# Seven block products in place of eight for half of the channel mixer's second product

## The chip, the cores and the metric

The kernel runs on one NeuronCore of a Trainium2 chip. The metric is the device time of one execution in microseconds (us), lower is better; the median of three runs stands for it.

## The reference

The reference is a trunk of two layers over 256 tokens of 2048 channels. What the change touches is the channel mixer that ends each token mixer:

```python
for i in range(DEPTH):                # DEPTH = 2, D_FF = 8192
    ...
    h = rms_norm(x, mlp_norm[i])
    x = x + jnp.square(jax.nn.relu(h @ mlp_w1[i])) @ mlp_w2[i]
    g = jax.nn.sigmoid(rms_norm(x, ple_norm[i]) @ ple_w_gate[i])
    x = x + g * (p[i] @ ple_w_proj[i])
return rms_norm(x, final_norm)
```

`mlp_w1` is 2048x8192 and `mlp_w2` 8192x2048 in each layer; tokens and weights are float32.

## The kernel before, in words

**Divided operands.** TensorE gets every float32 operand as a high part and a low part (type float32r), and each product is three passes: high by high, high by low, low by high (`PASSES_W_MOVES`). The class `Weights` streams the weights: a tile of 128x2048 float32 (1 MB: 512 rows by 512 columns of the matrix) is loaded by SyncE's DMA queue into a `raw` buffer (`load`, L61; three buffers), ScalarE copies it to the high half of an `hl` buffer (`divide`, L75; four buffers), and VectorE subtracts that from the raw tile to make the low half (L76). This pair is called a split below. `next` hands out the tiles in order and keeps three of them split ahead of the one in use. The order of TensorE's and SyncE's instructions is the order in which the code issues them; ScalarE's and VectorE's is set by the tile framework's scheduler when the program is built. Each engine runs its queue strictly in that order, and semaphores hold an instruction until its inputs are ready and its output buffer is free.

**The channel mixer.** The 8192 hidden channels are 16 chunks q of 512, taken in pairs f = 0 to 7. `w1` (L523, L528) makes a chunk in two PSUM tiles with the weights standing and the tokens moving; ScalarE and VectorE bring it out (L538 to L543): low columns added, relu, square, divided into a high and a low part `h`. `w2` multiplies a pair of chunks by the columns of `mlp_w2`, four column groups n of 512 channels, two weight tiles and 48 matmuls of 128x512 for each (`rows_product`, L297), and VectorE adds the PSUM result, scaled by the squared inverse norm, to the residual `x` (`add_to_x`, L320). The loop runs w1(f), then w2(f-1), so that TensorE always has a product whose inputs are old. After the last pair, `after.chunk(n)` squares the finished column group of x and, some matmuls later, transposes it on TensorE (L275) for the gate product of `embed` that comes next.

A **round** below is what TensorE does for one pair: two chunks of w1 (8 tiles) and the four column groups of w2 (8 tiles). There are 8 rounds in a layer and 16 in all.

## Time and profile before

| what | value |
|---|---|
| median of 3 runs (lowest, highest) | 1995.26 us (1995.0, 1995.62) |
| the profiled execution's own time | 1994.55 us |
| its span, first to last instruction | 1992.8 us |
| TensorE matmuls busy | 1972.8 us, 99% of the span, 9918 matmuls |
| VectorE busy | 1166.5 us, 59% |
| ScalarE busy | 932.2 us, 47% |
| weights read | 373.75 MB, 189 GB/s over the span |
| granted TensorE clock, mean | 0.998 of full speed |

The profile is of one execution. Busy time of an engine is the time in which an instruction of it runs; since matmuls are pipelined, a busy TensorE is not one at its peak. The view by lines groups equal instructions (busy us, mean ns of one, and what ended the idle time before them); the timeline has them in order of time; the chain is followed back from the last instruction to whatever released each step.

### The profile page before, as it was taken

Reading aid. Unit: us, or ns where it says so; the run is one execution under the profiler, and the core shown is the slowest. Engines: PE = TensorE matmul, PEld = TensorE weight load, DVE = VectorE, ACT = ScalarE, POOL = GpSimd, SP = SyncE. Lnnn points to the kernel's source line nnn. Section 1 sums busy time; section 2 is a strip of 40 time slices with the busy share of each in tenths; the row PEclk is TensorE's granted clock in tenths of the full one; section 3 lists DMA queues with packets and bytes.
Section 4 is the critical chain, followed back from the end, with each engine's and each line's share of the span. In section 5 each row is a group of like instructions: output and inputs, shape, how many; then the busy total and the mean of one; then the engine's idle time right before and its main releaser. Section 6 shows DMA issues by size and latency. Waiting matters only on the chain.

```text
span 1992.8 us, 23653 instructions
## 1 busy us (share of the span) xinstructions
PE 1972.8 (99%) x9918; PEld 1680.6 (84%) x9918; DVE 1166.5 (59%) x1213; ACT 932.2 (47%) x921; POOL 128.2 (6%) x65
## 2 busy tenths in 40 slices
PE   8999999999999999999999999999999999999997
PEld 6888888888888888888889888888888888888886
DVE  7988755555555555555656555555455455555654
ACT  6435555353444435354545445444435354444543
POOL 2875000000000000000001000000000000000000
PEclk9999999999999999999999999999999999999999
DMA  7645555555555555555453555555555555555543
GB/s 272 240 167 211 190 190 180 200 190 190 190 190 190 190 192 191 191 191 189 177 182 125 190 190 189 192 190 190 191 190 190 190 190 192 191 190 196 207 155 122
DMA packets 55659, 377.40 MB, mean 189 GB/s; under 512 B 6384, under 2 KB 6528, under 8 KB 11648
## 3 DMA queue, kind: packets, MB, share of 16 engines
q1 hardware_dynamic: 55152, 374.82, 52.2%
q8 instruction: 77, 1.26, 0.2%
q10 hardware_dynamic: 144, 1.05, 0.1%
q14 instruction: 30, 0.25, 0.0%
q0 software_dynamic: 256, 0.02, 0.0%
HBM read 373.75 MB, written 2.10 MB: 189 GB/s over the span
## 4 chain that ended last, share of the span: by engine, by line
PE 96%; DMA 1%; DVE 1%; issue 1%; POOL 0%; ACT 0%; SPq 0%; ACTq 0%; POOLq 0%; DVEq 0%
PE ps_o L297 35%; PE ps_h L523 23%; PE ps_h L528 12%; PE ps_g L297 9%; PE ps_od L297 4%; PE ps_out L297 3%; PE ps_pool L297 2%; PE ps_in L297 2%; PE ps_outp L297 1%; PE ps_e L297 1%; DMA raw<-in_w_in 1%; PE ps_f L310 1%; PE ps_z L639 1%; POOL hl L76 0%; DVE hl L76 0%
## 5 line engine op out<-in xcount | busy, mean ns | idle before, releaser
L76 DVE TENSOR_TENSOR hl<-raw,hl 128x2048 fp32r<-128x2048 f32 (+2 forms) x341 | 746.1, 2192 | 624.5 <-ACT hl L75 624.4
L75 ACT ACTIVATE hl<-raw 128x2048 fp32r<-128x2048 f32 (+3 forms) x369 | 673.7, 1830 | 830.1 <-PE ps_o L297 375.4
L297 PE MATMUL ps_o<-hl,h 128*128 128x512 f32 x3072 | 700.6, 389 | 0.0
L297 PEld LDWEIGHTS ps_o<-hl,h 128*128 128x128 f32 x3072 | 575.4, 188 | 118.6
L523 PE MATMUL ps_h<-xT_mlp,hl 128*128 128x512 f32 x2048 | 488.3, 390 | 0.0
L523 PEld LDWEIGHTS ps_h<-xT_mlp,hl 128*128 128x128 f32 x2048 | 377.3, 188 | 73.6
L528 PEld LDWEIGHTS ps_h<-xT_mlp,hl 128*128 128x128 f32 x2048 | 262.6, 191 | 10.0
L528 PE MATMUL ps_h<-xT_mlp,hl 128*128 128x256 f32 x2048 | 265.7, 283 | 0.0
L297 PE MATMUL ps_g<-hl,xT_ple 128*128 128x512 f32 (+1 forms) x816 | 177.6, 377 | 0.0
L297 PEld LDWEIGHTS ps_g<-hl,xT_ple 128*128 128x128 f32 x816 | 146.4, 188 | 28.2 <-DVE hl L76 0.4
L320 DVE SCALAR_TENSOR_TENSOR x<-ps_o,rstd,x 128x512 f32<-128x512 f32 x128 | 90.2, 746 | 69.9 <-PE ps_o L297 69.9
L76 POOL TENSOR_TENSOR hl<-raw,hl 128x2048 fp32r<-128x2048 f32 (+1 forms) x28 | 120.1, 4313 | 55.2 <-ACT hl L75 55.2
L297 PE MATMUL ps_in<-hl,xT_ev 128*128 128x512 f32 x384 | 90.6, 396 | 6.7 <-ACT hl L75 6.7
L394 DVE SCALAR_TENSOR_TENSOR acc<-vp,vT,acc 128x256 f32<-128x256 f32 x240 | 96.4, 481 | 0.1
L297 PEld LDWEIGHTS ps_in<-hl,xT_ev 128*128 128x128 f32 x384 | 72.4, 190 | 23.1 <-ACT hl L75 6.9
L297 PE MATMUL ps_od<-hl,f 128*128 128x512 f32 x384 | 88.3, 390 | 0.0
L297 PEld LDWEIGHTS ps_od<-hl,f 128*128 128x128 f32 x384 | 71.7, 188 | 15.1 <-issue 0.4
L538 ACT ACTIVATE relu<-ps_h 128x512 f32<-128x512 f32 x64 | 38.2, 598 | 97.7 <-PE ps_h L528 97.7
L539 DVE TENSOR_TENSOR relu<-ps_h,relu 128x512 f32<-128x512 f32 x64 | 44.3, 692 | 40.4 <-ACT relu L538 40.4
L653 POOL CAST top<-z 128x4 fp32r<-128x4 f32 x8 | 1.5, 189 | 895.0 <-DVE z L219 895.0
L297 PE MATMUL ps_out<-hl,y_conv 128*128 128x512 f32 x192 | 44.5, 391 | 0.0
L297 PE MATMUL ps_pool<-hl,xT_ev 128*128 128x512 f32 x192 | 44.5, 390 | 0.0
(142 smaller groups left out, 785.6 us busy)
## 6 DMA issues: line engine op xcount, KB each, us to landing
raw<-in_mlp_w SPq DMA_DIRECT2D x256, 1024.0 KB, 4.8
raw<-in_ple_w_gate SPq DMA_DIRECT2D x32, 1024.0 KB, 4.8
raw<-in_w_in SPq DMA_DIRECT2D x20, 1024.0 KB, 4.9
raw<-in_ev_w_out SPq DMA_DIRECT2D x16, 1024.0 KB, 4.8
raw<-in_od_w_out SPq DMA_DIRECT2D x16, 1024.0 KB, 4.9
raw<-in_w_in SPq DMA_DIRECT2D x16, 256.0 KB, 6.5
raw<-in_ple_w_proj SPq DMA_DIRECT2D x8, 512.0 KB, 3.6
x<-in_x SPq DMA_DIRECT2D x2, 1024.0 KB, 7.8
```

What stands on the lines that cost most here:

```text
L75: self.nc.scalar.activation(hl[:, 0, c], t[:, c], AF.Copy)
L76: getattr(self.nc, lo).tensor_tensor(hl[:, 1, c], t[:, c], hl[:, 0, c].bitcast(F32), ALU.subtract)
L297: nc.tensor.matmul(ps[t][:, cols], lhsT=acts[:, s, kt, t * P:(t + 1) * P], rhs=w[:, m, kt * 512 + cols.start:kt * 512 + cols.stop], start= ...
L310: nc.tensor.matmul(out_ps, lhsT=w[sw], rhs=act[sa], start=bank_first and i == 0, stop=i == n - 1, skip_group_check=True)
L320: nc.vector.scalar_tensor_tensor(xs, ps[:, t * 512:(t + 1) * 512], scale[:, t:t + 1], xs, ALU.mult, ALU.add)
L394: nc.vector.scalar_tensor_tensor(acc, src, cwT[:, ch, k:k + 1], acc, ALU.mult, ALU.add)
L523: nc.tensor.matmul(pss[p][:, e], lhsT=w[:, 0, ch], rhs=norm.xT[c][:, :, kt], start=c == 0 and kt == 0, stop=False, skip_group_check=True)
L528: nc.tensor.matmul(pss[p][:, e, 1], lhsT=w[:, 1, ch], rhs=norm.xT[c][:, 0, kt], start=False, stop=c == 3 and kt == 3, skip_group_check=True)
L538: nc.scalar.activation(r, pss[p][:, :, 1], AF.Copy)
L539: nc.vector.tensor_tensor(s, pss[p][:, :, 0], r, ALU.add)
L639: nc.tensor.matmul(ps[g][:, t], lhsT=norm.xT[c][:, s, 2 * g + k, t * P:(t + 1) * P], rhs=dft[:, m, k * 256:(k + 1) * 256], start=k == 0 an ...
L653: nc.gpsimd.tensor_copy(top[:, :, t, 2 * c:2 * c + 2], z[:, :, :, t, P])
```

## The change

Column groups 0 and 1 of the second product are now taken together as a 2x2 block product: the two token halves (128 each) by two halves of each 512-row chunk, times these row halves by the two column groups. Instead of eight block products of 128x256 by 256x512 there are seven (`pair`, Winograd's form of Strassen's scheme), each on a sum of blocks. Column groups 2 and 3 stay as they were.

- **Sums of weights.** For each chunk the tiles of column groups 0 and 1, x and y, stay in their raw buffers while `add_seven` forms the seven operands in place, as half tiles of 128x1024: four additions on VectorE (L102) and seven splits (L105, L106), where two whole tiles were split before. For a pair of chunks that is 8 additions and 14 half splits, packed into seven `hl` tiles. There are four raw buffers now, and a smaller scratch for DMA descriptors makes room.
- **Sums of tokens.** After each chunk of w1, four 128x256 differences and sums of hidden blocks (L605 to L608) are formed on VectorE and divided (L611, L612) into a tile `g` beside `h`.
- **The norm's scale** is applied to the hidden channels before the square, by a row `rows` (one small matmul per layer, L565), in the instruction that does the relu on VectorE (L597); the relu on ScalarE is gone, and `add_to_x` is a plain addition (L366).
- **Results.** Two of the seven products are added straight to x (L649, 128x1024; L657, 128x512); the other four PSUM halves are added to `sums` in SBUF in every round (L655, two of 128x1024; ScalarE copies them in the first, L653). After the last round `pair_end` combines `sums` into the four blocks of x with eight additions (L662).
- **Order.** A round is now: a chunk of w1, column group 2, the seven products, the next chunk of w1, column group 3. At the end of a layer the column groups are finished in the order 2, 0 and 1, 3.

Names used below for the tiles of a round in TensorE's order: W (two, column group 2), P1 to P7 (the seven tiles of half splits, P1a and P1b the halves of P1), A0 to A3 (w1), V (two, column group 3), B0 to B3 (w1 of the next round).

The diff, cut:

```diff
-RAW_BUFS = 3
+RAW_BUFS = 4
...
+    def add_seven(self, tiles):
+        q, parts = 1024, []
+        for x, y in tiles:
+            x, y = self.source(x), self.source(y)
+            parts += [
+                [("split", (x, 0))], [("split", (x, q))],
+                [("add", (x, 0), (y, 0)), ("split", (y, q))], [("split", (x, 0))],
+                [("add", (y, 0), (y, q)), ("split", (y, 0))], [("add", (x, 0), (y, q)), ("split", (x, 0))],
+                [("add", (x, 0), (x, q)), ("split", (x, 0))]]
+        for k in range(0, len(parts), 2):
+            self.made([step + ((i * q, q) if step[0] == "split" else (q,))
+                       for i, part in enumerate(parts[k:k + 2]) for step in part])
...
+        for i, (what, (r, c), other, w) in enumerate(steps):
+            src = self.raw[r][:, c:c + w]
+            if what == "add":
+                self.nc.vector.tensor_tensor(src, src, self.raw[other[0]][:, other[1]:other[1] + w], ALU.add)
+                continue
+            to = slice(other, other + w)
+            self.nc.scalar.activation(hl[:, 0, to], src, AF.Copy)
+            getattr(self.nc, lo).tensor_tensor(hl[:, 1, to], src, hl[:, 0, to].bitcast(F32), ALU.subtract)
...
+        def w2(f, n):
             for q in (2 * f, 2 * f + 1):
-                for c in range(4):
-                    ws.add(a["mlp_w1"][i, q, c])
-
-        def w2(f):
-            for n in range(4):
-                for c in (2 * f, 2 * f + 1):
-                    ws.add(a["mlp_w2"][i, n, c])
+                ws.add(a["mlp_w2"][i, n, q])
+        def pair(f):
+            ws.add_seven([(a["mlp_w2"][i, 0, q], a["mlp_w2"][i, 1, q]) for q in (2 * f, 2 * f + 1)])
         w1(0)
-        for f in range(1, 8):
-            w1(f)
-            w2(f - 1)
-        w2(7)
+        w1(1)
+        for f in range(8):
+            if f < 7:
+                w1(2 * f + 2)
+            w2(f, 2)
+            pair(f)
+            if f < 7:
+                w1(2 * f + 3)
+            w2(f, 3)
...
+        def scales():
+            diag = work.tile([P, S], F32, name="diag", tag="sr")
+            for t in range(2):
+                nc.vector.tensor_scalar(diag[:, t * P:(t + 1) * P], ident, norm.rstd[:, t:t + 1], None, ALU.mult)
+            ps = sm_pool.tile([P, S], F32, tag="sm", name=f"ps_rows{i}")
+            nc.tensor.matmul(ps, lhsT=ones, rhs=diag, start=True, stop=True)
+            nc.scalar.activation(rows, ps, AF.Copy, scale=float(DC))
...
+                with tc.high_priority(offset=PRIO):
+                    nc.scalar.activation(r, pss[p][:, :, 1], AF.Copy)
+                    nc.vector.tensor_tensor(s, pss[p][:, :, 0], r, ALU.add)
+                nc.vector.scalar_tensor_tensor(r, s, 0.0, rows.unsqueeze(1).broadcast_to([P, 2, S]), ALU.max, ALU.mult)
+                nc.scalar.activation(s, r, AF.Square)
+                nc.scalar.activation(h[:, 0, e], s, AF.Copy)
+                nc.vector.tensor_tensor(h[:, 1, e], s, h[:, 0, e].bitcast(F32), ALU.subtract)
+                ss.append(s)
+            g = act_pool.tile([P, 2, 4, 2, P], F32R, tag="act", name=f"g{i}_{q}")
+            a11, a21, a12, a22 = ss[0][:, :, :P], ss[0][:, :, P:], ss[1][:, :, :P], ss[1][:, :, P:]
+            u, v = (work.tile([P, 2, 2, P], F32, name=f"form{k}", tag="sr") for k in range(2))
+            nc.vector.tensor_tensor(v[:, 0], a11, a21, ALU.subtract)
+            nc.vector.tensor_tensor(u[:, 0], a22, a21, ALU.subtract)
+            nc.vector.tensor_tensor(u[:, 1], a11, u[:, 0], ALU.add)
+            nc.vector.tensor_tensor(v[:, 1], a12, u[:, 1], ALU.subtract)
+            for k, src in enumerate((u, v)):
+                to = slice(2 * k, 2 * k + 2)
+                nc.scalar.activation(g[:, 0, to], src, AF.Copy)
+                nc.vector.tensor_tensor(g[:, 1, to], src, g[:, 0, to].bitcast(F32), ALU.subtract)
+            hidden[q], forms[q] = h, g
...
-                add_to_x(ps, n, rstd2)
...
+        def w2(f, n):
+            ps = psum_mm(f"ps_o{i}_{f}_{n}")
             for q in (2 * f, 2 * f + 1):
-                pss = [psum_mm(f"ps_h{i}_{q}{p}").rearrange("p (e s n) -> p e s n", e=2, s=2) for p in range(2)]
-                for c in range(4):
-                    w = ws.next()
-                    blocks = [(p, e, kt, slice(kt * 512 + (2 * p + e) * P, kt * 512 + (2 * p + e + 1) * P))
-                              for p in range(2) for e in range(2) for kt in range(4)]
-                    for p, e, kt, ch in blocks:
-                        nc.tensor.matmul(pss[p][:, e], lhsT=w[:, 0, ch], rhs=norm.xT[c][:, :, kt],
-                                         start=c == 0 and kt == 0, stop=False, skip_group_check=True)
-                        if kt == 3 and e == 1:
-                            tick()
-                    for p, e, kt, ch in blocks:
-                        nc.tensor.matmul(pss[p][:, e, 1], lhsT=w[:, 1, ch], rhs=norm.xT[c][:, 0, kt],
-                                         start=False, stop=c == 3 and kt == 3, skip_group_check=True)
-                        if kt == 3 and e == 1:
-                            tick()
-                h = act_tile(f"h{i}_{q}")
-                for p in range(2):
-                    e = slice(2 * p, 2 * p + 2)
-                    r = work.tile([P, 2, S], F32, name="relu", tag="sr")
-                    s = work.tile([P, 2, S], F32, name="relu2", tag="sv")
-                    with tc.high_priority(offset=PRIO):
-                        nc.scalar.activation(r, pss[p][:, :, 1], AF.Copy)
-                        nc.vector.tensor_tensor(s, pss[p][:, :, 0], r, ALU.add)
-                    nc.scalar.activation(r, s, AF.Relu)
-                    nc.scalar.activation(s, r, AF.Square)
-                    nc.scalar.activation(h[:, 0, e], s, AF.Copy)
-                    nc.vector.tensor_tensor(h[:, 1, e], s, h[:, 0, e].bitcast(F32), ALU.subtract)
-                hidden[q] = h
-
-        def w2(f):
-            for n in range(4):
-                ps = psum_mm(f"ps_o{i}_{f}_{n}")
-                for q in (2 * f, 2 * f + 1):
-                    rows_product(ps, hidden[q], range(4), q == 2 * f, q == 2 * f + 1)
-                add_to_x(ps, n, rstd2)
-                if f == 7:
-                    after.chunk(n)
-
+                rows_product(ps, hidden[q], range(4), q == 2 * f, q == 2 * f + 1)
+            add_to_x(ps, n)
...
+        def pair(f):
+            p15, p76, p23 = psum_mm(f"ps_s{i}_{f}a"), None, psum_mm(f"ps_s{i}_{f}b")
+            p4 = sm_pool.tile([P, 512], F32, tag="sm", name=f"ps_s{i}_{f}d")
+            k = 0
+            for q in (2 * f, 2 * f + 1):
+                h, g = hidden[q], forms[q]
+                for what in range(7):
+                    if k % 2 == 0:
+                        w = ws.next()
+                    if what == 4 and p76 is None:
+                        p76 = psum_mm(f"ps_s{i}_{f}c")
+                    out_ps = (lambda: p15[:, :512], lambda: p23[:, :512], lambda: p23[:, 512:], lambda: p15[:, 512:],
+                              lambda: p76[:, :512], lambda: p76[:, 512:], lambda: p4)[what]()
+                    for kt in range(2):
+                        for m, (s, j) in enumerate(PASSES_W_MOVES):
+                            act = (h[:, s, kt, :P], h[:, s, 2 + kt, :P], g[:, s, 3, kt], g[:, s, 0, kt],
+                                   g[:, s, 2, kt], g[:, s, 1, kt], h[:, s, 2 + kt, P:])[what]
+                            col = (k % 2) * 1024 + kt * 512
+                            nc.tensor.matmul(out_ps, lhsT=act, rhs=w[:, j, col:col + 512],
+                                             start=q % 2 == 0 and kt == 0 and m == 0,
+                                             stop=q % 2 == 1 and kt == 1 and m == 2)
+                    tick()
+                    k += 1
+                    if q % 2 == 0:
+                        continue
+                    if what == 2:
+                        nc.vector.tensor_tensor(x[:, 0, :1024], p23, x[:, 0, :1024], ALU.add)
+                    elif what in (3, 5):
+                        ps, to = (p15, sums[:, :1024]) if what == 3 else (p76, sums[:, 1024:])
+                        if f == 0:
+                            nc.scalar.activation(to, ps, AF.Copy)
+                        else:
+                            nc.vector.tensor_tensor(to, ps, to, ALU.add)
+                    elif what == 6:
+                        nc.vector.tensor_tensor(x[:, 1, :512], p4, x[:, 1, :512], ALU.add)
+        def pair_end():
+            m1, m5, m7, m6 = (sums[:, k * 512:(k + 1) * 512] for k in range(4))
+            c11, c12, c21, c22 = (x[:, t, n * 512:(n + 1) * 512] for t in range(2) for n in range(2))
+            add, sub = ((lambda to, p, q, op=op: nc.vector.tensor_tensor(to, p, q, op)) for op in (ALU.add, ALU.subtract))
+            add(c11, c11, m1)
+            sub(m6, m6, m1)
+            sub(c21, c21, m6)
+            add(c21, c21, m7)
+            after.chunk(0)
+            sub(m5, m6, m5)
+            add(c12, c12, m5)
+            add(c22, c22, m5)
+            sub(c22, c22, m7)
+            after.chunk(1)
+        put_off(scales, 10)
         w1(0)
-        rstd2 = small.tile([P, 2], F32, name=f"rstd2_{i}", tag="rstd2")
-        nc.vector.tensor_tensor(rstd2, norm.rstd, norm.rstd, ALU.mult)
-        for f in range(1, 8):
-            w1(f)
-            w2(f - 1)
-        w2(7)
+        w1(1)
+        for f in range(8):
+            if f < 7:
+                w1(2 * f + 2)
+            w2(f, 2)
+            if f == 7:
+                after.chunk(2)
+            pair(f)
+            if f == 7:
+                pair_end()
+            else:
+                w1(2 * f + 3)
+            w2(f, 3)
+            if f == 7:
+                after.chunk(3)
...
-        pT = act_pool.tile([P, 2, 2, S], F32R, tag="pT", name=f"pT{i}", bufs=1)
+        pT = act_pool.tile([P, 2, 2, S], F32R, tag="act", name=f"pT{i}")
...
-    nc = _bacc.Bacc("TRN2", target_bir_lowering=False, num_devices=1)
+    nc = _bacc.Bacc("TRN2", target_bir_lowering=False, num_devices=1, dynamic_dma_scratch_size=2048)
```

What the built program's queues look like: `hl_N` is a split tile, `raw_N` a loaded one, `h_q` and `g_q` the hidden chunk and its sums, `ps_...` a PSUM tile.

TensorE in round f = 4 of the first layer, before, the second product of one pair:

```order
L297 MATMUL ps_o_4_0_5095<-hl_4969,h_8_4333 128x512 x24
L297 MATMUL ps_o_4_0_5095<-hl_5006,h_9_4500 128x512 x24
L297 MATMUL ps_o_4_1_5156<-hl_5043,h_8_4333 128x512 x24
L297 MATMUL ps_o_4_1_5156<-hl_5098,h_9_4500 128x512 x24
L297 MATMUL ps_o_4_2_5217<-hl_5127,h_8_4333 128x512 x24
L297 MATMUL ps_o_4_2_5217<-hl_5159,h_9_4500 128x512 x24
L297 MATMUL ps_o_4_3_5278<-hl_5188,h_8_4333 128x512 x24
L297 MATMUL ps_o_4_3_5278<-hl_5220,h_9_4500 128x512 x24
```

and now, the seven products of the same pair, from P1 on to the end of P7a (hl_5074 is P1, hl_5269 is P7):

```order
L641 MATMUL ps_s_4a<-hl_5074,h_8_4490 128x512 x6
L641 MATMUL ps_s_4b<-hl_5074,h_8_4490 128x512 x6
L641 MATMUL ps_s_4b<-hl_5142,g_8_4507 128x512 x6
L641 MATMUL ps_s_4a<-hl_5142,g_8_4507 128x512 x6
L641 MATMUL ps_s_4c<-hl_5174,g_8_4507 128x512 x12
L641 MATMUL ps_s_4d<-hl_5210,h_8_4490 128x512 x6
L641 MATMUL ps_s_4a<-hl_5210,h_9_4872 128x512 x6
L641 MATMUL ps_s_4b<-hl_5228,h_9_4872 128x512 x6
L641 MATMUL ps_s_4b<-hl_5228,g_9_4889 128x512 x6
L641 MATMUL ps_s_4a<-hl_5248,g_9_4889 128x512 x6
L641 MATMUL ps_s_4c<-hl_5248,g_9_4889 128x512 x6
L641 MATMUL ps_s_4c<-hl_5269,g_9_4889 128x512 x6
```

A tile of the second product lasted 24 matmuls; a tile of the seven lasts 12, six for each half. With the one row not shown, the pair's column groups 0 and 1 take 84 matmuls in place of 96.

VectorE beside these products, before (L76 splits a whole tile, L320 adds a column group to x):

```order
L76 TENSOR_TENSOR hl_5127<-raw_5041,hl_5127 128x2048
L320 SCALAR_TENSOR_TENSOR x<-ps_o_4_0_5095,rstd_0_2447,x 128x512 x2
L76 TENSOR_TENSOR hl_5159<-raw_5096,hl_5159 128x2048
L76 TENSOR_TENSOR hl_5188<-raw_5125,hl_5188 128x2048
L320 SCALAR_TENSOR_TENSOR x<-ps_o_4_1_5156,rstd_0_2447,x 128x512 x2
```

and now, the last twelve instructions up to the split of P7b (hl_5290 is A0; raw_5140 and raw_5172 are the tiles x and y of the second chunk):

```order
L102 TENSOR_TENSOR raw_5140<-raw_5140,raw_5172 128x1024
L106 TENSOR_TENSOR hl_5228<-raw_5172,hl_5228 128x1024
L102 TENSOR_TENSOR raw_5172<-raw_5172 128x1024
L106 TENSOR_TENSOR hl_5248<-raw_5140,hl_5248 128x1024
L106 TENSOR_TENSOR hl_5248<-raw_5172,hl_5248 128x1024
L102 TENSOR_TENSOR raw_5140<-raw_5140,raw_5172 128x1024
L649 TENSOR_TENSOR x<-ps_s_4b,x 128x1024
L106 TENSOR_TENSOR hl_5269<-raw_5140,hl_5269 128x1024
L655 TENSOR_TENSOR sums<-ps_s_4a,sums 128x1024
L102 TENSOR_TENSOR raw_5140<-raw_5140 128x1024
L106 TENSOR_TENSOR hl_5290<-raw_5246,hl_5290 128x2048
L106 TENSOR_TENSOR hl_5269<-raw_5140,hl_5269 128x1024
```

Between two half splits there are additions of weights, and ahead of the last half split, which P7b waits for, there stand two additions of PSUM results and the whole split of the next w1 tile.

VectorE at the end of the first layer's mixer, where hl_7016 is the second V tile and hl_7034, hl_7070 and hl_7137 are the first three tiles of the gate product:

```order
L106 TENSOR_TENSOR hl_7016<-raw_6975,hl_7016 128x2048
L655 TENSOR_TENSOR sums<-ps_s_7a,sums 128x1024
L106 TENSOR_TENSOR hl_7034<-raw_6996,hl_7034 128x2048
L655 TENSOR_TENSOR sums<-ps_s_7c,sums 128x1024
L657 TENSOR_TENSOR x<-ps_s_7d,x 128x512
L662 TENSOR_TENSOR x<-x,sums 128x512
L662 TENSOR_TENSOR sums<-sums 128x512
L106 TENSOR_TENSOR hl_7070<-raw_7014,hl_7070 128x2048
L662 TENSOR_TENSOR x<-x,sums 128x512
L662 TENSOR_TENSOR sums<-sums 128x512
L662 TENSOR_TENSOR x<-x,sums 128x512 x3
L106 TENSOR_TENSOR hl_7137<-raw_7032,hl_7137 128x2048
```

The additions that finish column groups 0 and 1 stand among the splits of three later tiles; TensorE's transposes of these column groups are queued between the two V tiles.

## Rows read from the trace of the kernel before

**Rows 1.** The page: busy time by engine, then shares of the chain by engine.

```profile
PE 1972.8 (99%) x9918; PEld 1680.6 (84%) x9918; DVE 1166.5 (59%) x1213; ACT 932.2 (47%) x921; POOL 128.2 (6%) x65
...
PE 96%; DMA 1%; DVE 1%; issue 1%; POOL 0%; ACT 0%; SPq 0%; ACTq 0%; POOLq 0%; DVEq 0%
```

**Rows 2.** Chain of waits in order of time: start us, us, what; two successive rounds.

```profile
1264.83 43.55 PE ps_o L297 x192
1352.88 43.55 PE ps_o L297 x192
```

**Rows 3.** Timeline of one round: start us, us, engine, line, instruction, [idle before <-releaser].

```profile
791.67 1.92 ACT L75 ACTIVATE hl<-raw 128x2048 fp32r<-128x2048 f32 x1 [3.44 <-PE ps_o L297]
791.68 1.41 DVE L320 SCALAR_TENSOR_TENSOR x<-ps_o,rstd,x 128x512 f32<-128x512 f32 x2 [1.12 <-PE ps_o L297]
793.62 2.29 DVE L76 TENSOR_TENSOR hl<-raw,hl 128x2048 fp32r<-128x2048 f32 x1 [0.54 <-ACT hl L75]
...
829.65 3.82 PE L523 MATMUL ps_h<-xT_mlp,hl 128*128 128x512 f32 x16
829.85 1.92 ACT L75 ACTIVATE hl<-raw 128x2048 fp32r<-128x2048 f32 x1 [3.62 <-PE ps_h L528]
...
835.22 3.82 PE L523 MATMUL ps_h<-xT_mlp,hl 128*128 128x512 f32 x16
```

**Rows 4.** Busy time by stretch, the same round: stretch, us, PE, PEld, DVE, ACT, ...

```profile
780.57:868.62 88.05, 88.05 (x450) 75.39 (x449) 47.48 (x33) 39.09 (x32) 0.00 (x0) 1.00 0.53 191
```

**Rows 5.** Timeline of VectorE in the first stage, instructions that follow each other without idle.

```profile
13.82 2.50 DVE L76 TENSOR_TENSOR hl<-raw,hl 128x512 fp32r<-128x512 f32 x4
16.34 1.23 DVE L343 TENSOR_TENSOR x_in<-x_in,x_in 128x1024 f32<-128x1024 f32 x1
17.48 1.67 DVE L219 SCALAR_TENSOR_TENSOR xT_ev<-x_in,vT,xT_ev 128x256 fp32r<-128x256 f32 x4
...
27.74 4.48 DVE L76 TENSOR_TENSOR hl<-raw,hl 128x2048 fp32r<-128x2048 f32 x2
```

**Rows 6.** VectorE by lines and shapes: xcount | busy us, mean ns | idle before <-releaser.

```profile
L76 DVE TENSOR_TENSOR hl<-raw,hl 128x1024 fp32r<-128x1024 f32 x2 | 2.4, 1218 | 0.0
...
L469 DVE TENSOR_TENSOR y_conv<-sg,y_conv 128x256 fp32r<-128x256 f32 x8 | 3.0, 412 | 0.0
...
L448 DVE TENSOR_TENSOR ln_sq<-ln_sq 128x512 f32<-128x512 f32 x1 | 0.7, 692 | 0.0
```

**Rows 7.** ScalarE by lines and shapes.

```profile
L75 ACT ACTIVATE hl<-raw 128x1024 fp32r<-128x1024 f32 x2 | 2.1, 1060 | 4.1 <-PE ps_g L297 4.1
```

**Rows 8.** DMA issues: tensor, queue, count, KB each, median us from issue to landing.

```profile
raw<-in_mlp_w SPq DMA_DIRECT2D x256, 1024.0 KB, 4.8
```

**Rows 9.** TensorE by lines: the small product with the matrix `ones`.

```profile
L440 PE MATMUL ln_mean<-csum,ones 128*128 128x256 f32 x4 | 1.0, 378 | 0.0
```

**Rows 10.** Timeline of TensorE at the end of the first layer's mixer, before.

```profile
899.70 28.95 PE L297 MATMUL ps_o<-hl,h 128*128 128x512 f32 x127
928.49 1.03 PE L275 MATMUL tr_ple<-ident,x 128*128 128x128 f32 x8
929.28 11.16 PE L297 MATMUL ps_o<-hl,h 128*128 128x512 f32 x48
```

**Rows 11.** TensorE's last matmuls (timeline), then stretches behind them (columns as in Rows 4, then clock).

```profile
1975.75 6.88 PE L297 MATMUL ps_g<-hl,xT_ple 128*128 128x256 f32 x56
...
1985.00:1986.00 1.00, 0.00 (x0) 0.00 (x0) 0.82 (x6) 0.00 (x0) 0.00 (x0) 1.00 0.00 0
1986.00:1986.50 0.50, 0.00 (x0) 0.00 (x0) 0.40 (x3) 0.00 (x0) 0.00 (x0) 0.83 0.00 0
1986.50:1987.00 0.50, 0.00 (x0) 0.00 (x0) 0.40 (x4) 0.00 (x0) 0.00 (x0) 0.50 0.00 0
```

71 lines of the change are left out of this document (52 added, 19 removed).

## The prediction

> **What bounds the kernel now.** I read the page first: TensorE is busy for 1972.8 of the 1992.8 us, and 96% of the chain that ended last is TensorE's [rows 1]. So a matmul taken away is worth its time only while something else does not come to bound. The chain of waits in order of time gives the pace: 192 matmuls of 128x512 in 43.55 us, 0.2268 us each, and the same row comes again 88.05 us later, one round [rows 2]. The timeline of a round shows how the others hang on it: ScalarE starts a copy 0.20 us after TensorE has left a tile, VectorE subtracts 0.03 us after the copy, and a w1 tile takes 835.22 - 829.65 = 5.57 us [rows 3]. In a round of 88.05 us VectorE is busy for 47.5 us and ScalarE for 39.1 [rows 4]: both have room on average. The question is whether VectorE has room just where the seven products run, since the additions and the three extra half splits per chunk all fall there.
>
> **What is saved.** 12 of 96 matmuls per round: 12 x 0.2268 = 2.72 us, 43.5 us in 16 rounds. That is all TensorE can give.
>
> **VectorE's prices.** Instructions that stand behind each other without a wait start a little before the one ahead has ended. Four 128x512 take 2.50 us, so (2.50 - 0.69) / 3 = 0.60 us from start to start; a 128x1024 addition in place holds the queue for 17.48 - 16.34 = 1.14 us although it lasts 1.22; two whole splits take 4.48 us, 2.19 apart; four scalar_tensor_tensor of 128x256 take 1.67 us, 0.40 apart [rows 5]. Alone, a 128x1024 split lasts 1.22 us, 128x512 0.69 and 128x256 0.41, 0.08 over its share of the queue [rows 6]; so 0.33 for a 128x256. The two scalar_tensor_tensor of 128x512 take 1.41 us [rows 3], 0.70 each.
>
> [...]
>
> **The queue of one round.** Let 0 be the moment when TensorE begins W. P1 takes the buffer of the tile four before it, free at -5.57; with 0.20 us, ScalarE's copy of a half tile (1.06 us [rows 7]) and 0.03, VectorE starts P1a at -4.3. From there to P7b its queue holds 14 half splits, 8 additions of weights, two of PSUM results (L649, L655), 24 in all at 1.14; one whole split (A0) at 2.19; the w1 chunk's two scalar_tensor_tensor at 0.70 and six instructions of 128x512 at 0.60; two of column group 2 at 0.60; four 128x256 at 0.33. Sum 27.4 + 2.2 + 1.4 + 4.8 + 1.3 = 37.1 us, and 0.2 where one needs the result just ahead: P7b is ready at 33.0. TensorE would be there after 48 matmuls of W and 13 half tiles of six, (48 + 78) x 0.2268 = 28.6. **It waits 4.4 us**, against 2.72 saved: a round is 1.7 us longer.
>
> Nothing else starves this queue: buffers come free earlier than VectorE asks (P5's at 13.6, VectorE there at 17), ScalarE has under 25 us of work in those 37 us (14 copies of 1.06, two of 1.92 [rows 3, 7] and eight small ones), and a raw buffer is free four tiles before its use, at 5.57 us a tile of w1, for a load of 4.8 us [rows 8]. After P7b VectorE catches up during A0 to A3 (22 us for about 9 us of splits), so every round starts alike.
>
> **First and last round.** In a layer's first round ScalarE copies `sums`, one 1.14 less ahead of P7b: a wait of 3.3 us. In the last there is no w1 chunk around the products, and VectorE is paced by column group 2 up to 11.1; behind it stand 13 of 1.14, two of 0.60, four of 0.40 and A0's counterpart, the first V tile, at 2.19, with waits between ScalarE and VectorE of 0.6: P7b at 31.5, TensorE there at 28.6 and 0.8 for eight transposes (929.28 - 928.49 [rows 10]), a wait of 2.1. Then what finishes column groups 0 and 1 is late. The first gate tile's load can start only when P7b has freed its raw buffer: 31.5 + 4.8 + 1.92 + 2.29 = 40.5 when VectorE has split it, and behind it stand L655, L657, two L662, another whole split and four L662, 1.14 + 0.6 + 1.2 + 2.19 + 2.6: 48.2. TensorE has ended its first V tile at 31.5 + 1.36 + 5.44 = 38.3 and stands before the transposes: 9.9 us; column group 1 needs an addition, a whole split and the last addition more, 51.7, and with 0.8 of transposes between it waits 2.6. Together 14.6 us, where before it waited for nothing [rows 10].
>
> **Sum.** Per layer 3.3 + 6 x 4.4 + 14.6 = 44.3 us of waits against 8 x 2.72 = 21.8 saved: 22.5, 45.0 for both. The product that makes `rows` adds 0.4 per layer [rows 9]. The relu that ScalarE loses, the plain addition in L366 and the fourth raw buffer I cost at nothing: they lie beside TensorE, and bytes are the same. The profiled execution's own time is 1994.55 us, its span 1992.8, and it lies 0.04% below the median of 1995.26; 1994.55 + 45.8 gives **2040 us**.
>
> **Bounds.** The one unknown is how densely VectorE's queue runs with semaphores between halves that ScalarE has just copied. Whole lengths (24 x 1.22 + 2.29 + 10 x 0.69 + 4 x 0.41 + 0.2 = 40.3) put P7b at 36.0, a wait of 7.4; with 6.2 in the first round and about 17.6 in the last, 2088. The densest reading takes only the slope of rows 5, 2.19 - 1.14 = 1.05 per 1024 elements: 33.6 us, a wait of 0.8, none in the first round and 12 in the last: 1985. I take the middle value, since rows 5 show that very pattern, splits and additions in one queue.
>
> **Rivals.**
> 1. *VectorE keeps up* (faster). If P7b comes at 28.6, the waits in the rounds are gone and about 12 us per layer are left at the end: 1994.55 - 43.5 + 24 = 1975 us. It decides at a mean wait of 1.0 us per round (14 rounds, 29.2 of 43.5 us used up by the ends), a queue 3.4 us shorter than summed. For it: VectorE's 47.5 us per round [rows 4], to which some 25 us come (14 of 1.14, 4 x 0.70, 4 x 0.60, 8 x 0.33 and 1 more for PSUM results), still fit into 85. Against: they are not spread over the round, and the lengths in rows 5 and 6 hardly vary.
> 2. *No overlap* (slower): 2088 us, above. Against it rows 5.
> 3. *The clock falls in the waits.* [...] If P7b and A0 then run at half speed, up to 1.36 + 5.57 = 6.9 us more in each of 14 places, and at least nothing; half of that is 48 us, so 2088 us. For it: the length of the waits. Against: there is one fall in the trace, and no row shows matmuls behind it. [...]
>
> That the change does not do what it says I leave out: the queue shows 84 matmuls.
>
> **How the numbers follow.** About 0.2%, 4 us, is what a measurement of this kernel can tell. Forecast (waits of 2.5 to 6 us per round) 0.60, rival 1 0.13, rival 2 0.10, rival 3 0.12, and 0.05 for waits that just eat the saving. So faster 0.13, same 0.05, slower 0.82. The range reaches from just below the time that eats the saving to just above rivals 2 and 3: 1996 to 2095 us. Left out are rival 1 and the far end of 3.
>
> **What would show it.** In the profile after: 84 matmuls of 128x512 for the seven products in a round of about 89.8 us; idle time of TensorE before P7b's matmuls (line 641) of about 4.4 us, ended by VectorE's L106; VectorE nearly without idle from P1a to P7b; some 12 us idle before the transposes at each layer's end; 128x1024 splits of 1.22 us, starting 1.14 apart. If TensorE goes through the products without idle, the queue sum is wrong; if the waits are there but the clock row falls below 1.00 behind them, rival 3 adds to it.

## The result, and the profile after

The changed kernel takes 2072.86 us (median of 4 runs, 2070.65 to 2076.8) beside 1995.15 us for the kernel before (4 runs, 1995.0 to 1995.62): 1.0391 times as long, 95% interval 1.0373 to 1.0409. The forecast was 2040 us with a range of 1996 to 2095: the direction is right, the time is inside the range, and the forecast is 33 us too low. The profiled execution took 2070.65 us with a span of 2068.9, 76.1 us more than the span before.

On the page, busy time by engine and then the chain by engine answer to [rows 1]:

```profile
PE 1977.0 (96%) x9730; PEld 1668.3 (81%) x9730; DVE 1564.3 (76%) x1771; ACT 1039.6 (50%) x1087; POOL 128.9 (6%) x65
...
PE 69%; DVE 27%; issue 2%; ACT 2%; DMA 0%; ACTq 0%; SPq 0%
```

TensorE has 188 matmuls less and is busy 4.2 us longer; VectorE is busy 397.8 us more, and 27% of the chain is now VectorE's. The first matmuls of the seven products start, by the view of the tile `ps_s_<f>a` of the first layer, at 330.6, 419.4, 510.9, 602.9, 695.0, 787.1 and 879.2 us: 88.8 us for the first round, 91.5 for the second and 92.0 to 92.1 for the next four, where it was 88.05 [rows 2]. The busy time in one of them (columns as in [rows 4]):

```profile
602.90:694.98 92.08, 88.46 (x437) 74.62 (x436) 71.71 (x67) 45.55 (x43) 0.00 (x0) 0.96 0.50 183
```

VectorE has 71.7 us of work in 92.1 and is no bound on average. Where it is late, TensorE's timeline of the same round shows (start us, us, instruction, idle before and what ended it); 617.86 is P5b and P6b, 622.90 and 625.15 are P7b, 627.45 is A0:

```profile
617.86 3.11 PE L641 MATMUL ps_s_3c<-hl,g 128*128 128x512 f32 x12
622.90 0.56 PE L641 MATMUL ps_s_3d<-hl,h 128*128 128x512 f32 x1 [1.92 <-ACT hl L105]
625.15 2.50 PE L641 MATMUL ps_s_3d<-hl,h 128*128 128x512 f32 x5 [1.69 <-DVE hl L106]
627.45 5.03 PE L580 MATMUL ps_h<-xT_mlp,hl 128*128 128x512 f32 x16
632.32 2.08 PE L585 MATMUL ps_h<-xT_mlp,hl 128*128 128x256 f32 x16
```

At 0.2268 us each, the 12 matmuls ahead end at 617.86 + 2.72 = 620.58. P7b's second matmul, the first that reads VectorE's half, starts at 625.15 and not at 620.81: **4.34 us late**. Then 21 matmuls take 632.32 - 625.15 = 7.17 us where 4.76 are due: **2.41 us more**. The windows over this stretch (the number ahead of the last two is the granted clock) show why:

```profile
621.00:623.00 2.00, 0.10 (x1) 0.10 (x1) 2.00 (x2) 2.00 (x3) 0.00 (x0) 1.00 0.07 29
623.00:624.00 1.00, 0.46 (x1) 0.08 (x1) 1.00 (x2) 1.00 (x1) 0.00 (x0) 0.60 0.00 0
624.00:630.00 6.00, 4.85 (x11) 3.80 (x12) 6.00 (x4) 1.59 (x2) 0.00 (x0) 0.50 0.85 306
630.00:631.00 1.00, 1.00 (x6) 0.81 (x5) 1.00 (x2) 0.98 (x1) 0.00 (x0) 0.99 0.99 418
```

TensorE ran one matmul between 621 and 625; the granted clock fell from 1.00 to 0.50 and was back at 0.99 from 630 on. The round is thus 88.05 - 2.72 + 4.34 + 2.41 = 92.08 us, to the hundredth what the window has.

VectorE's timeline says what it did meanwhile: P1a first, then, without idle up to P7b, the rows below; 621.67 holds A0's whole split, P7b's half, A1 and A2.

```profile
587.73 2.36 DVE L106 TENSOR_TENSOR hl<-raw,hl 128x1024 fp32r<-128x1024 f32 x2 [2.42 <-ACT hl L105]
...
619.41 1.22 DVE L655 TENSOR_TENSOR sums<-ps_s_3a,sums 128x1024 f32<-128x1024 f32 x1
620.54 1.22 DVE L102 TENSOR_TENSOR raw<-raw 128x1024 f32<-128x1024 f32 x1
621.67 7.82 DVE L106 TENSOR_TENSOR hl<-raw,hl 128x2048 fp32r<-128x2048 f32 x4
```

The end of the first layer's mixer, which answers to [rows 10], on TensorE:

```profile
968.83 0.39 PE L641 MATMUL ps_s_7d<-hl,h 128*128 128x512 f32 x1
969.92 1.43 PE L641 MATMUL ps_s_7d<-hl,h 128*128 128x512 f32 x5 [0.70 <-DVE hl L106]
971.18 5.61 PE L345 MATMUL ps_o<-hl,h 128*128 128x512 f32 x24
977.78 0.33 PE L323 MATMUL tr_ple<-ident,x 128*128 128x128 f32 x1 [1.00 <-DVE x L662]
982.39 1.76 PE L323 MATMUL tr_ple<-ident,x 128*128 128x128 f32 x7 [4.28 <-DVE x L662]
988.18 1.94 PE L323 MATMUL tr_ple<-ident,x 128*128 128x128 f32 x8 [4.04 <-DVE xT_ple L267]
989.78 6.69 PE L345 MATMUL ps_o<-hl,h 128*128 128x512 f32 x24
996.31 5.61 PE L345 MATMUL ps_g<-hl,xT_ple 128*128 128x512 f32 x24
```

From the last pair's first matmul at 949.14 to the first gate matmul at 996.31 it takes 47.2 us, where 132 matmuls and 24 transposes (0.79 per eight [rows 10]) are 32.3: 14.9 us lost. SyncE's loads and two rows of VectorE there, for the account further down (973.12 is the split of the first gate tile):

```profile
962.97 9.45 SPq L89 DMA_DIRECT2D raw<-in_ple_w_gate  x4
973.12 2.28 DVE L106 TENSOR_TENSOR hl<-raw,hl 128x2048 fp32r<-128x2048 f32 x1
981.66 1.89 DVE L662 TENSOR_TENSOR x<-x,sums 128x512 f32<-128x512 f32 x3
```

### The profile page after: what moved, and what is told of

The parts are those of the page before. It is cut to its first block, busy times and chain, and to the rows that moved or that the text cites. A ratio compares the mean times of both kernels' runs of the same rounds, so it can differ in the third digit from the quotient of the medians.

```text
span 2068.9 us, 24040 instructions
## 1 busy us (share of the span) xinstructions
PE 1977.0 (96%) x9730; PEld 1668.3 (81%) x9730; DVE 1564.3 (76%) x1771; ACT 1039.6 (50%) x1087; POOL 128.9 (6%) x65
## 4 chain that ended last, share of the span: by engine, by line
PE 69%; DVE 27%; issue 2%; ACT 2%; DMA 0%; ACTq 0%; SPq 0%
PE ps_h L580 21%; DVE hl L106 14%; PE ps_h L585 11%; PE ps_o L345 9%; PE ps_g L345 8%; DVE raw L102 7%; PE ps_od L345 4%; PE ps_in L345 4%; PE ps_out L345 3%; PE ps_pool L345 2%; ACT hl L105 2%; PE ps_outp L345 1%; PE ps_e L345 1%; DVE h L600 1%; DVE g L612 1%
## 5 line engine op out<-in xcount | busy, mean ns | idle before, releaser
L105 ACT ACTIVATE hl<-raw 128x2048 fp32r<-128x2048 f32 (+2 forms) x529 | 774.7, 1491 | 769.0 <-PE ps_h L585 315.8
L106 DVE TENSOR_TENSOR hl<-raw,hl 128x2048 fp32r<-128x2048 f32 (+3 forms) x501 | 865.5, 1744 | 381.5 <-ACT hl L105 379.8
L580 PE MATMUL ps_h<-xT_mlp,hl 128*128 128x512 f32 x2048 | 503.6, 399 | 0.0
L580 PEld LDWEIGHTS ps_h<-xT_mlp,hl 128*128 128x128 f32 x2048 | 391.1, 194 | 80.4
L345 PE MATMUL ps_o<-hl,h 128*128 128x512 f32 x1536 | 356.3, 391 | 0.0
L345 PEld LDWEIGHTS ps_o<-hl,h 128*128 128x128 f32 x1536 | 288.0, 189 | 58.7
L585 PEld LDWEIGHTS ps_h<-xT_mlp,hl 128*128 128x128 f32 x2048 | 262.6, 191 | 10.0
L106 POOL TENSOR_TENSOR hl<-raw,hl 128x2048 fp32r<-128x2048 f32 (+1 forms) x28 | 120.8, 4328 | 55.8 <-ACT hl L105 55.8
L345 PEld LDWEIGHTS ps_od<-hl,f 128*128 128x128 f32 x384 | 71.8, 188 | 14.8
L102 DVE TENSOR_TENSOR raw<-raw 128x1024 f32<-128x1024 f32 x64 | 78.0, 1219 | 0.7
L102 DVE TENSOR_TENSOR raw<-raw,raw 128x1024 f32<-128x1024 f32 x64 | 78.0, 1218 | 0.1
L596 DVE TENSOR_TENSOR relu<-ps_h,relu 128x512 f32<-128x512 f32 x64 | 42.7, 685 | 17.9 <-ACT relu L595 17.9
L611 ACT ACTIVATE g<-form 128x512 fp32r<-128x512 f32 x64 | 38.4, 623 | 24.4 <-DVE form L608 13.4
```

The lines of the kernel that those rows point to most:

```text
L102: self.nc.vector.tensor_tensor(src, src, self.raw[other[0]][:, other[1]:other[1] + w], ALU.add)
L105: self.nc.scalar.activation(hl[:, 0, to], src, AF.Copy)
L106: getattr(self.nc, lo).tensor_tensor(hl[:, 1, to], src, hl[:, 0, to].bitcast(F32), ALU.subtract)
L345: nc.tensor.matmul(ps[t][:, cols], lhsT=acts[:, s, kt, t * P:(t + 1) * P], rhs=w[:, m, kt * 512 + cols.start:kt * 512 + cols.stop], start= ...
L580: nc.tensor.matmul(pss[p][:, e], lhsT=w[:, 0, ch], rhs=norm.xT[c][:, :, kt], start=c == 0 and kt == 0, stop=False, skip_group_check=True)
L585: nc.tensor.matmul(pss[p][:, e, 1], lhsT=w[:, 1, ch], rhs=norm.xT[c][:, 0, kt], start=False, stop=c == 3 and kt == 3, skip_group_check=True)
```

## The experiments

Two questions were open: is it VectorE's queue that sets the wait, and is it the clock that takes the rest? Ratios are to runs of the kernel before on the same chip.

### e1: no additions

```
-                self.nc.vector.tensor_tensor(src, src, self.raw[other[0]][...], ALU.add)
                 continue
```

> Left out: the eight additions of weight blocks of each pair (the blocks are split as they were loaded, so the seven products are of other matrices). Everything else stays. Theory 1 (VectorE's queue from the first half split of a pair to the last one is what TensorE waits for): without 8 x 1.14 = 9.1 us the last half split of a steady round is ready about 24 us after the round's start instead of 33.1, ahead of TensorE at 28.6, so the wait and the fall of the clock behind it go, a steady round takes 88.06 - 2.72 = 85.3 us instead of 92.1, and the time is 1995 - 43.5 plus some microseconds that stay at the two ends of layer: 1953 to 1965 us. Rival (the wait is for ScalarE's half splits or for the loads of the weights): the round stays over 90 us and the time above 2040 us.

Measured: 1980.47 us, ratio 0.9928 (0.9913 to 0.9943). The steady round is what theory 1 says, TensorE without idle at a granted clock of 1.00:

```profile
587.60:673.00 85.40, 85.40 (x438) 73.19 (x438) 62.89 (x58) 45.78 (x42) 0.00 (x0) 1.00 0.56 198
```

The wait and the fall of the clock behind it come from the additions on VectorE; the run takes out at once their place in the queue and the stops behind them, while ScalarE has to copy a sum. The time is 15 us above what was expected, and that lies at the ends of the layers, each of which still loses 13 to 14 us by the starts of its matmuls; the transposes wait as before:

```profile
938.11 0.98 PE L322 MATMUL tr_ple<-ident,x 128*128 128x128 f32 x7 [4.28 <-DVE x L661]
943.91 1.94 PE L322 MATMUL tr_ple<-ident,x 128*128 128x128 f32 x8 [4.81 <-DVE xT_ple L266]
```

9.1 us here, 9.3 in the changed kernel: these waits do not hang on the additions of weights.

### e2: the additions on GpSimd

```
-                self.nc.vector.tensor_tensor(src, src, ...)
+                self.nc.gpsimd.tensor_tensor(src, src, ...)
```

> The eight additions of weight blocks of each pair go from VectorE to GpSimd. In the kernel before GpSimd took 4.3 us for a subtraction of 128x2048, so an addition of 128x1024 should take about 2.2 us, 17 us per round of GpSimd, which is idle there. Theory 1 (VectorE's queue): VectorE's queue is 9.1 us shorter per pair, the last half split is ready before TensorE comes to it, the round takes about 85.3 us, the time is 1953 to 1970 us. Rival A (the additions in a chain: three of them on one block with splits between, 3 x (2.2 + 2.2) = 13.2 us per pair of tiles, too slow on GpSimd): TensorE waits some microseconds at the last products of each half of a pair, 1990 to 2060 us. Rival B (VectorE's operations get longer while GpSimd works beside it): the 1024 operations take more than 1.22 us and the gain is less than half, 2010 us or more.

Measured: 2197.7 us, ratio 1.1016 (1.0999 to 1.1032), far above every case; a round takes 99.0 us. GpSimd's additions take 3.6 and 2.7 us and not 2.2 (the 4.3 us that this came from is a mean of two shapes; GpSimd's subtractions took 4.63 for 128x2048 and 2.42 for 128x1024 in the kernel before), and several of VectorE's operations on SBUF get longer (lines by shape, mean ns):

```profile
L102 POOL TENSOR_TENSOR raw<-raw,raw 128x1024 f32<-128x1024 f32 x64 | 233.0, 3641 | 1207.5 <-DVE hl L106 1207.5
L102 POOL TENSOR_TENSOR raw<-raw 128x1024 f32<-128x1024 f32 x64 | 173.1, 2705 | 81.5 <-DVE hl L106 79.0
L106 DVE TENSOR_TENSOR hl<-raw,hl 128x1024 fp32r<-128x1024 f32 x232 | 367.1, 1609 | 151.7 <-ACT hl L105 151.0
L597 DVE SCALAR_TENSOR_TENSOR relu<-relu,rows 128x512 f32<-128x512 f32 x64 | 73.5, 1149 | 1.7
L596 DVE TENSOR_TENSOR relu<-ps_h,relu 128x512 f32<-128x512 f32 x64 | 43.9, 686 | 42.8 <-ACT relu L595 42.8
```

The half splits took 1221 ns on average in the changed kernel and L597 688. Rivals A and B hold together: the chain of additions is longer, and operations of both engines last longer; how much each of the two takes is not shown. Theory 1 is not tested by this run.

### e3: work in the wait

```
+                    if k == 13 and 0 < f < 7:
+                        spare = sm_pool.tile([P, 512], F32, tag="sm", name=f"spare{i}_{f}")
+                        for _ in range(14):
+                            nc.tensor.matmul(spare, lhsT=h[:, 0, 0, :P], rhs=w[:, 0, :512], start=True, stop=True)
```

> In rounds 1 to 6 of each layer 14 matmuls of 512 columns, 14 x 0.227 = 3.2 us, into a spare PSUM tile that nobody reads, stand on TensorE ahead of the pair's last product, where it waits 4.4 us for VectorE; the rest stays. Theory (the clock falls because TensorE stands still there, and that costs about 2.3 us of a round): the last product starts as late as before, 33.1 us after the round's start, but it and the 16 matmuls behind it run at the full clock (3.8 us for these 16 and not 5.1), a round takes 89.8 us instead of 92.1, and 12 rounds give 28 us: 2045 us, within 6. Rival (what comes behind the wait is slow for another reason, as the next weight tile's split): no change, 2073 us, or up to 2085 where the added matmuls delay the last product.

Measured: 2046.72 us, ratio 1.026 (1.0245 to 1.0275): 26 us less than the changed kernel, for added work that nobody reads. A steady round takes 89.8 us. TensorE's timeline and the windows at the same place:

```profile
621.26 3.34 PE L639 MATMUL spare<-hl,h 128*128 128x512 f32 x14
624.44 0.39 PE L645 MATMUL ps_s_3d<-hl,h 128*128 128x512 f32 x1
625.60 1.43 PE L645 MATMUL ps_s_3d<-hl,h 128*128 128x512 f32 x5 [0.77 <-DVE hl L106]
626.87 3.79 PE L580 MATMUL ps_h<-xT_mlp,hl 128*128 128x512 f32 x16
```

```profile
620.00:624.00 4.00, 4.00 (x19) 3.31 (x19) 4.00 (x3) 4.00 (x4) 0.00 (x0) 1.00 0.42 176
624.00:630.00 6.00, 5.23 (x23) 4.04 (x22) 6.00 (x5) 1.66 (x2) 0.00 (x0) 1.00 0.72 272
```

VectorE is as late as before, but the granted clock stays at 1.00 and A0's first 16 matmuls take 3.8 us in place of 5.0. The theory of the clock holds with its size; its rival, a slow A0 for another reason, falls.

### e4 and e6: the end of a layer

In e4 the last pair goes ahead of column group 2; in e6 only the transposes and the sums move.

```
 e4                                             e6
-            w2(f, 2)                           -            after.chunk(0)
+            if f < 7:                          +            with tc.high_priority(offset=PRIO):
+                w2(f, 2)                       +                ... the eight sums ...
             pair(f)                            +            after.chunk(0, 6)
+            if f == 7: pair_end(); w2(f, 2)    +            after.chunk(1, 8)
```

> In the last round of each layer the pair goes ahead of both single column groups, so that 10.9 us of products of column group 2 stand between the pair's end and the transposes that need its sums, in place of 0. Theory (the last round loses about 14 us, mostly because the transposes wait for the sums of the pair, and the clock falls there): the waits ahead of the transposes shrink by 5 to 10 us a layer, less 1 to 4 us by which the pair's splits come later, since a column group no longer runs ahead of them: 2073 - 8 to - 16, 2057 to 2065 us. Rival (the same VectorE queue sets the end in either order, and the wait only moves into the pair): no change, 2069 to 2077 us.

> Only the end of a layer: the transposes of column groups 0 and 1 are put off from 24 matmuls behind the pair to 36 and 48 matmuls, and the sums of the pair get priority on VectorE. Theory (at the end of a layer TensorE waits 9.3 us because the transposes stand on its queue ahead of 24 matmuls that need nothing from the pair; the run without additions waited 9.1 us there too, so it is their place and the chain of eight sums, not the queue of additions): the 24 matmuls that stood behind them cover 5.4 us, the clock falls less, so 5 to 9 us less a layer, 2073 - 10 to - 18: 2055 to 2063 us. Rival (the wait moves on to the first gate product, which needs the turned and scaled column group 0): under 3 us less a layer, 2067 to 2073 us.

Measured: e4 2077.56 us, ratio 1.0414 (1.0397 to 1.0432); e6 2074.05, 1.0398 (1.0381 to 1.0415). Neither gains; both rivals hold. In e4 the wait goes into the pair, whose splits no longer have a column group ahead of them; P7b of the last round:

```profile
960.76 0.50 PE L644 MATMUL ps_s_7d<-hl,h 128*128 128x512 f32 x1 [1.93 <-ACT hl L105]
963.01 2.01 PE L644 MATMUL ps_s_7d<-hl,h 128*128 128x512 f32 x5 [1.74 <-DVE hl L106]
```

In e6 the waits ahead of the transposes are 2.74 and 4.94 us: the transposes come later, and so does the scaling that frees their PSUM tiles.

### e5: eight products in the changed order

```
-            pair(f)
-            if f == 7: pair_end()
+            for n in range(2):
+                w2(f, n)
```

> The changed kernel with eight products: column groups 0 and 1 are made as before (96 matmuls each and round, no additions of weight blocks or token blocks, no sums at the end), in the changed order of a round, with the scaling by rows on VectorE and the order of loads as changed. Theory (what costs time belongs to the seven products: their half splits, additions and sums; the new order and the scaling by rows are hidden): 1993 to 1999 us, that is 1995 and up to 0.8 us for the two products that make the row of scales. Rival (a part of the loss belongs to the order of the round or to VectorE's added scaling, 2 x 0.69 us per first product): 2005 to 2030 us.

Measured: 1996.39 us, ratio 1.0011 (1.0001 to 1.002). The order of the round and the scaling by rows cost about 2 us, by the interval 4 at most; the loss belongs to the seven products.

### e7 and e8: the token side later

```
+            if q > 1 and q % 2 == 0:
+                put_off(tokens, 22)      # lines 597 to 612
+            else:
+                tokens()
...
+        with in_order():                 # VectorE and ScalarE as written
             for f in range(8):
```

> In the rounds of the mixer VectorE and ScalarE work in the order in which the program is written, and for the first product made ahead of a round's column group 2 the scaling, squaring, splitting and sums of token blocks (4 x 0.60 + 4 x 0.34 + 2 x 0.60 = 5.0 us of VectorE) are written behind the pair, so that they and the split of the next round's first weight tile (2.2) and the sums out of PSUM (2.3) stand behind the pair's last half split and not ahead of it. Theory (the queue ahead of the last half split is what counts): it is ready 5.0 + 2.2 + 2.3 = 9.5 us sooner, 23.6 us after the round's start, or up to 28 where VectorE now waits for ScalarE's half splits (1.06 each), ahead of TensorE at 28.6; a steady round takes 85.3 us as in the run without additions; 12 x 6.8 + 2 x 3.5 = 88 us less: 1985 us, 1979 to 1995. Rival (the fixed order makes VectorE stand still at each addition until ScalarE has split, as much as was gained): a round of 89 us or more, 2030 us or more.

> The fixed order with the token side later, and the transposes at the end of a layer put off to 36 and 48 matmuls behind the pair with the sums first. Theory: both gains add, 1985 - 10 to - 18: 1967 to 1975 us, faster than the kernel before (1995). Rival (in the fixed order the sums and the scaling at the end of a layer wait in line behind splits): no gain over the run with the token side later alone, 1980 to 1995 us.

Measured: e7 2152.33 us, ratio 1.0788 (1.0772 to 1.0804); e8 2147.31, 1.0767 (1.0751 to 1.0783). e7's rival holds. e8 is 5 us under e7, where 10 to 18 were expected of the later transposes; the times that both of its sides gave rested on e7's theory. VectorE's timeline ahead of P7b in e7 shows the stops: an addition, ScalarE's half split of its result, and only then VectorE's half. Six of the eight additions of a round are followed by such a stop, of 1.12 to 1.21 us:

```profile
635.06 1.23 DVE L102 TENSOR_TENSOR raw<-raw 128x1024 f32<-128x1024 f32 x1
637.41 1.23 DVE L106 TENSOR_TENSOR hl<-raw,hl 128x1024 fp32r<-128x1024 f32 x1 [1.12 <-ACT hl L105]
```

The round began at 605.31, so P7b is ready at 33.3, as late as in the changed kernel. In the changed kernel VectorE had no idle time there, so what stood between (A0's split, the token side) filled such stops: taking work out of the queue helps only if what is left can run without them.

### e9 to e12: a version without the wait

e9 is e7 with each addition written ahead of the split before it; e11 also holds A0's split back until two sums out of PSUM are written and leaves the last round to the scheduler; e10 and e12 put the transposes off on top.

```
 e9   [add(x, 0, y, 0), split(y, q, 0), add(y, 0, y, q), split(x, 0, q), add(x, 0, y, q)],
      [split(y, 0, 0), split(x, 0, q), add(x, 0, x, q)], ...
 e11  k, ws.hold = 0, ws.used + 7 if f < 7 else 10 ** 6    # until the first sum of p15 is written
 e12  after.chunk(2, 19); after.chunk(0, 8); after.chunk(1, 11); after.chunk(3, 8)
```

> As the run with the token side later in a fixed order, but each addition of weight blocks is written one or two half splits ahead of the split that needs its result, so that ScalarE's half split (1.06) runs beside another operation of VectorE. Theory (what cost there was that VectorE stood still 1.1 to 1.2 us behind seven of the eight additions, and that the sums out of PSUM came late behind the last half split): the last half split is ready after 14 + 8 operations of 1.14, four of 0.60 and one stop of 1.1, 28.6 us from 4.3 us ahead of the round's start, that is at 24.3, ahead of TensorE at 28.6, and PSUM is free in time; a steady round takes 85.3 us, the clock stays up in it, and the time is as in the run without additions or some microseconds above, 1980 to 1992 us: faster than the kernel before (1995). Rival (the fixed order stops VectorE elsewhere, as at the rows and forms of the token side): a round over 89 us, 2030 us or more.

> As the run with the additions written ahead, and at the end of a layer the transposes of column groups 2, 0 and 1 are put off to 6, 36 and 48 matmuls behind the pair, with the sums ahead. Theory: there is less to wait for at the end of a layer, since the last half split of the last pair is early too and column group 2's transposes do not stop the pair: 3 to 8 us a layer less than in the run with the additions ahead alone, 1966 to 1984 us. Rival (the scaling of the transposed groups then comes later than the first gate product needs it): the same time as that run, or up to 6 us more.

Measured: e9 2049.08 us, ratio 1.0274 (1.0258 to 1.0289); e10 2054.01, 1.0296 (1.0278 to 1.0313). P7b is ready at 27.6 us of the round and TensorE goes through all seven products, but a round still takes 88.8 us, since the next product waits for PSUM that late sums free, which neither side had said. TensorE at A0 in e9, the sum, and the clock over this stretch:

```profile
611.81 1.52 PE L652 MATMUL ps_s_3d<-hl,h 128*128 128x512 f32 x6
615.02 2.08 PE L582 MATMUL ps_h<-xT_mlp,hl 128*128 128x512 f32 x8 [1.69 <-ACT hl L107]
618.26 2.11 PE L582 MATMUL ps_h<-xT_mlp,hl 128*128 128x512 f32 x8 [1.17 <-DVE sums L666]
613.66 1.22 DVE L660 TENSOR_TENSOR x<-ps_s_3b,x 128x1024 f32<-128x1024 f32 x1
608.00:622.00 14.00, 11.14 (x55) 8.91 (x54) 12.29 (x9) 6.47 (x4) 0.00 (x0) 1.00 0.82 291
```

The first wait is put down to ScalarE, whose split was long done; the sum L660 that frees the buffer of P2 and P3 ended at 614.88, and e11, which puts the sums first, is rid of most of this wait. e10's later transposes gain nothing, as its rival has it.

> As the run with the additions ahead, with two changes: the split of the next round's first weight tile is held back until the pair's first two sums out of PSUM (column groups 0 and 1 of the first token half; M1 and M5) are written, so that these stand directly behind the last half split; and the fixed order ends with round 6, the last round of a layer is ordered by the scheduler as in the changed kernel. Theory (in that run a steady round lost 88.8 - 85.3 = 3.5 us only because the next first product waited 1.69 and 1.17 us for PSUM that those two sums free, and the fixed order cost some 12 us at each end of layer): the first sum ends about 1.2 us behind the last half split (27.6 after the round's start), 28.8, and the second at 30, as TensorE leaves the pair; a steady round takes 85.3 to 85.9 us and the ends of layer cost what they cost in the changed kernel: 2073 - 12 x 6.5 - 2 x 3.4 = 1988 us, 1979 to 1996: faster than the changed kernel by 4 per cent and than the kernel before by 0 to 0.8 per cent. Rival (the held split then comes too late for the first product of the next round): a round of 87 to 89 us, 2005 to 2035 us.

> As the run before in this list, and at the end of a layer the transposes of column groups 2, 0 and 1 are put off to 30, 48 and 66 matmuls behind the pair (group 1 into the first gate product), those of group 3 by 24 more, with their scaling ahead on VectorE and ScalarE. Theory (what TensorE waits for at the end of a layer is the chain from the pair's end over the sums to the scaled column group 0, some 14 us, and only 10.9 us of products that need nothing of it are there): about 3 us of wait are left of 9.3, and the clock falls less, 4 to 8 us a layer less: 10 to 14 us under the run before in this list, 1974 us, 1966 to 1984. Rival (the scaling of group 0 comes later still, behind splits for the gate): no gain, as in the run with the transposes later.

Measured: e11 2008.53 us, ratio 1.0069 (1.0056 to 1.0083); e12 1993.74, 0.9995 (0.9986 to 1.0004). The steady round is 85.9 to 86.0 us in both, at the upper end of what was expected, and the clock 1.00 in it. The times are above what was expected because the last round of a layer got worse: in e11 P4 waits 7.87 us for the scaling of column group 2, which frees its PSUM tile, and in e12, where that is gone, the last pair waits twice for its splits, ahead of P4 (shown second) and of P7b (1.73 and 1.75 us):

```profile
929.40 2.90 PE L652 MATMUL ps_s_7d<-hl,h 128*128 128x512 f32 x6 [7.87 <-DVE xT_ple L269]
```

```profile
921.77 0.50 PE L656 MATMUL ps_s_7d<-hl,h 128*128 128x512 f32 x1 [1.57 <-ACT hl L107]
924.09 1.59 PE L656 MATMUL ps_s_7d<-hl,h 128*128 128x512 f32 x5 [1.82 <-DVE hl L108]
```

e12 is 14.8 us under e11, but three waits changed at once, so how much of it the later groups 0 and 1 gave stays open. It is 3.8% faster than the changed kernel and no different from the kernel before: the 43.5 us that the seven products save are used up again, 12 x 0.6 of them in the steady rounds and some 32, by the starts of the matmuls, at the two ends of the layers; the last 2 or 3 are not accounted for. No version here beats the kernel before with the whole computation in it.

## Why the prediction was right, and where it was not

The direction and its main cause, VectorE's queue ahead of P7b, were right. That the time lies inside the range is owed to the range, which reached up to rivals 2 and 3; the sum itself was 33 us low, and most of that is a term that it left at nothing.

- **What is saved.** 2.72 us a round: e1's round of 85.33 (85.3 to 85.4 between starts) is 88.05 - 2.72. Right.
- **VectorE's prices.** 1024-element operations took 1218 to 1221 ns and start 1.13 apart (619.41, 620.54, 621.67; forecast 1.14). Right.
- **The queue of a round.** P1a at 587.73, 4.27 us ahead of W (forecast 4.3); TensorE is 4.34 us late at P7b (forecast 4.4). Right: VectorE has no idle time between the two, and e1 shows that without the additions the wait is gone. That the queue as summed was not made of work alone, since the fillers in it covered ScalarE's half splits, the prediction did not see; e7 shows it.
- **What failed is the step from the wait to the round: "a round is 1.7 us longer".** It takes every matmul behind the wait at 0.2268 us. The fall of the clock stood apart as rival 3, with a chance of 0.12 and a price of 48 us, because no row showed matmuls behind a fall. It happened in each of the 12 steady rounds. By the starts of the matmuls it cost 2.35 to 2.49 us in ten of them and 1.75 in the second round of each layer, 28.0 in all: inside rival 3's 0 to 6.9 a place, and under the half of it that its 48 us took. e3, which keeps the clock up, shows that the fall is the cause. With it the 12 rounds lose 47.5 us net of what they save, 27.3 more than forecast. The first round of a layer is 0.7 us over 88.05 in the first layer (forecast 0.6) and 2.4 in the second (its seven products begin at 1291.4 and 1381.8), where the clock fell too: 1.9 more for the pair. With 0.6 for the two last rounds, 45.8 + 27.3 + 1.9 + 0.6 = 75.6, against 76.1 in the spans.
- **The last round.** Forecast 14.6 us of waits, 14.9 lost, but that is luck: errors cancel. The idle time ahead of P7b is 0.70 (forecast 2.1), ahead of column group 0's transposes 1.00 + 4.28 (9.9), ahead of column group 1's 4.04 (2.6); 0.84 ahead of P4, which waited for a scaling, had no term, and neither had the remaining 4.0, about 3 of it the slower clock (granted 0.50 from 982 to 990) and the rest the ends of matmuls that the view counts as busy. The 9.9 came from a load: the first gate tile's was to start only behind P7b's half split and its own split to end at 40.5 of the round. It was issued at 962.97, 24.7 us into the round that began at 938.26 (949.14 less 48 x 0.2268) and ahead of that half split, and its split ended at 37.1 (973.12 + 2.28); so group 0 was finished at about 44.1 and not at 48.2. Group 1's transposes were released by the scaling L267, which frees their PSUM tiles, and not by the sums. e1 still has 9.1 of the 9.3 us, as rival 1 had it with 12 us left per layer; which link of the chain from the pair's end over sums, gate splits and scaling sets them no run shows, since e4 and e6, which moved parts of it, gained nothing.
- **Costed at nothing** (relu, order, the fourth raw buffer): e5, 1.8 us over the median of the runs before on its chip, with 0.8 forecast for the rows. Right within the noise.
- **Rivals.** 1 (VectorE keeps up, 1975) did not come; e1 shows the time it would have given, 1980. 2 (no overlap) fell: the starts are 0.08 to 0.09 us before the ends (619.41 + 1.22 against 620.54). 3 (the clock) came in every steady round, on top of the forecast and at less than its price. The half speed that it takes for P7b and A0 is the 0.50 of [rows 11]; in the changed kernel the granted clock was 0.50 from 624 to 630, behind a wait.

## What to carry to other kernels

An engine that is busy for 72 of 92 us can still be the bound where a change puts all its new work: sum its queue between two deadlines, not over a round. A wait on TensorE can cost more than its length: here the 21 matmuls behind one of 4.34 us took 2.41 us more, most of them at a granted clock of 0.50. Give the matmuls behind such a wait a price at the lower clock in the sum, or keep TensorE busy through it (14 matmuls into a spare tile per round gave back 26 us). Before taking work out of a queue, check whether it fills stops that another engine causes (in e7 VectorE stood still 1.12 to 1.21 us behind six of eight additions).
